# A decoder-mixer kernel whose instruction order a list scheduler sets: VectorE and GpSimd take turns at SBUF in its plan, the last two G blocks run side by side over k, and the first output chunk is split ahead of the last output weights

## The chip, the core and the metric

The kernel runs on one core of a Trainium2 chip. A core has TensorE (PE in the profile; PEld is its weight load), VectorE (DVE), ScalarE (ACT), GpSimd (POOL), and SyncE (SP), which issues transfers; 16 DMA engines move data between HBM and the on-chip memory SBUF. TensorE writes its products to PSUM, eight banks of 128 x 512 floats here. Each engine executes its own instructions strictly in the order in which they stand in the program, and an instruction that waits for another engine holds up everything behind it on its own. The metric is the device time of one execution in microseconds; the median of the timed runs counts.

## The reference, cut to what matters

One layer over x of 1024 tokens by 1024 channels: a normalisation, one input projection, three mixers in parallel, one output projection, a second normalisation, and x added back. All inputs are float32.

```python
h = rms_norm(x, pre_norm_w)
z, xbc, dt_raw, q, f_raw, i_in, g, u, s5_gate = split(h @ w_in)
y_ssd  = ssd_mixer(z, xbc, dt_raw, ...)     # conv, 8 chunks of 128 tokens, 16 heads, gate by silu(z)
y_hgrn = hgrn2_mixer(q, f_raw, i_in, g, ..) # gated linear recurrence, 4 heads, gate by silu(g)
y_s5   = s5_mixer(u, s5_gate, ...)          # complex diagonal state space, then y @ glu_w, rms_norm
mix = concatenate([y_ssd, y_hgrn, y_s5])    # 1024 + 512 + 512 channels
x = x + rms_norm(mix @ w_out, post_norm_w)
```

## The kernel before

**Products.** The large matrix products are done in split precision: `split` (line 305) rounds a float32 tile to a high part on ScalarE (`act`, Copy) and subtracts to get a low part (`sub`), on GpSimd for weights and on VectorE for most others; `mm3` then issues three matmuls (high x high, high x low, low x high). Names of tiles begin with their pool: `r` (16 tiles) holds the normalised input `hh`, `hl` (high and low for eight k blocks), and later the first output weights; `v` (8 half tiles) holds split projection weights, and later the split mixer outputs; `w` holds raw weights; `s` the late weights; `x`, `m`, `h` are work tiles; `p` and `c` are the PSUM banks, four each, taken in turn. Projections write `p` banks, the mixers' small products write `c` banks.

**Stages.** `begin` (351) loads and splits the input and makes the sum of its squares (VectorE adds eight tiles into `m_111`; a matmul with `ones` then sums over partitions). The string `PLAN` (1405) emits in program order the projections (`u`, `x`, `a`, `g`, `z`), values (`v`), HGRN heads (`h`), S5 batches (`s`, with `o` the second half of one) and SSD chunks (`c`). Then follow the S5 output product `s5_glu`, the remaining `z` and `g` projections, and the output stage. In `stage_xbc` (519) the convolution is three `scalar_tensor_tensor` on VectorE (`x<-x,conv_w,x`, 128x1023, 128x1022 and 128x1021). In `s5_core` (978) VectorE runs eight scans, then two products (`pr`, and one half of `pi`) while GpSimd does the other half of `pi` (64x1016), and one add; `s5_emit` (1021) multiplies the result on TensorE.

**The end.** `stage_g2(2)` (487) makes the last two G blocks, each for the two halves n of the tokens: for every n first all eight k of the one block, then of the other. Each half goes through silu to `gs_d` in HBM and is read back in `out_gate` (1271). Then `wout` (751) loads, scales and splits the first eight output weights into the `r` tiles that held `hh` and `hl`: a copy on ScalarE and a `scalar_tensor_tensor` on VectorE each. `out_final` (1278) does one chunk of 128 tokens: it splits four half tiles (gated HGRN, rows 8 of w_out; S5, rows 12; the two halves of SSD, rows 0 and 4) into `v` tiles, each followed by its products with both column halves.

**What sets the order.** Nothing is executed in the order in which it is emitted. Each engine handle is wrapped (`Engine`, line 30; its helper makes line 38 the line of every instruction in the profile), so that `book` records all instructions. `depends` (105) finds which step needs which, and `arrange` (145) plays the program through with a length for each step (`Step`, 73): among all engines it always takes the step that can begin first, and of those that are ready the one with the highest rank; a switch of the matmul kind or of the activation table lowers the rank. It writes down the order on each engine, and `force` makes that the order of the program. So a length in `Step` that is wrong for the chip never makes a wrong result, but puts an instruction ahead of others that could have run while it waits. The plan of before charges a VectorE step `150 + n / 0.96` ns and a GpSimd step `120 + 2.3 * n` ns for n elements per partition, whatever the other engine does.

## Time and profile before

| | |
|---|---|
| median of the timed runs | 921.29 us |
| profiled execution, whole | 916.63 us |
| its span, first to last instruction | 914.7 us |
| mean granted TensorE clock | 0.988 |
| matmuls in the trace | 5857 |
| bytes read from and written to HBM | 89.52 MB, 34.18 MB |

The profile divides the span by engine (share of it in which the engine works), tells for each wait who ended it, and lists instructions in order of time. Nearly all instructions have line 38, so groups are told apart by the tiles that they write and read. A busy TensorE is what limits this kernel for most of the span; its idle time, and the stretches in which its clock was granted at less than 1, are what an order can change.

### The profile page before, as it was taken

The numbers are of one execution on the slowest core, as the hardware profiler recorded it, in microseconds if no ns is written. First come the engines' busy times: TensorE is split into PE (matmuls) and PEld (weight loads), VectorE is DVE, ScalarE is ACT, GpSimd is POOL, SyncE is SP. The second block draws the span as 40 slices with busy tenths as digits, with TensorE's granted clock in tenths as the row PEclk, the third lists the DMA queues.
The fourth block names the chain that finished last, engine by engine and source line by source line (L and its number), as shares of the span: only waits on it lengthen the run. The fifth ranks groups of instructions, "written<-read, shape, count | busy, mean of one in ns | idle before, by whom it ended". The sixth has DMA issues, their size and how long they took to land.

```text
span 914.7 us, 14969 instructions
## 1 busy us (share of the span) xinstructions
PE 865.6 (95%) x5857; PEld 713.3 (78%) x5857; DVE 615.4 (67%) x1069; ACT 380.8 (42%) x626; POOL 278.3 (30%) x232
## 2 busy tenths in 40 slices
PE   7999999898999989799998999999999799999997
PEld 5678878788978868578876877778878688888886
DVE  6997668978157589886857286796466755554531
ACT  5432434343134433254164786736354622222210
POOL 2551222553151135512423153452143231111100
PEclk9999999999999999999999999999999999999999
DMA  8132011472222422245556685778565744343200
GB/s 285 24 110 70 26 48 59 119 241 67 52 79 79 128 78 87 80 122 163 167 168 195 209 292 164 237 214 296 186 200 152 233 163 128 133 138 108 88 34 29
DMA packets 92792, 124.68 MB, mean 136 GB/s; under 512 B 9457, under 2 KB 65457, under 8 KB 92722
## 3 DMA queue, kind: packets, MB, share of 16 engines
q1 hardware_dynamic: 81634, 99.02, 34.4%
q10 hardware_dynamic: 11088, 24.71, 9.0%
q8 instruction: 46, 0.75, 0.3%
q14 instruction: 24, 0.20, 0.1%
HBM read 89.52 MB, written 34.18 MB: 135 GB/s over the span
## 4 chain that ended last, share of the span: by engine, by line
PE 43%; DVE 5%; ACT 2%; DMA 1%; issue 1%; POOL 0%; SPq 0%; DVEq 0%; ACTq 0%; POOLq 0%
PE p L38 32%; PE c L38 11%; DVE m L38 3%; DVE r L38 1%; DMA m<-na_d 1%; DMA m<-us_d 1%; ACT m L38 1%; DVE x L38 0%; DVE h L38 0%; ACT L38 0%; POOL h L38 0%; SPq L38 0%; ACT x L38 0%; ACT h L38 0%; DMA ys_d<-m 0%
## 5 line engine op out<-in xcount | busy, mean ns | idle before, releaser
L38 PE MATMUL p<-r,v 128*128 128x512 f32 (+1 forms) x2280 | 551.4, 395 | 7.6 <-ACT r L38 5.8
L38 PEld LDWEIGHTS p<-r,v 128*128 128x128 f32 x2280 | 420.4, 189 | 97.0 <-issue 6.1
L38 POOL TENSOR_TENSOR v<-w,v 128x512 fp32r<-128x512 f32 x76 | 109.6, 1445 | 218.7 <-ACT v L38 203.4
L38 ACT ACTIVATE v<-w 128x512 fp32r<-128x512 f32 x84 | 52.5, 631 | 174.5 <-PE p L38 163.1
L38 DVE TENSOR_TENSOR m<-m,m 128x512 f32<-128x512 f32 (+7 forms) x107 | 95.8, 918 | 9.9 <-POOL m L38 2.3
L38 PE MATMUL p<-s,v 128*128 128x512 f32 (+1 forms) x408 | 94.5, 389 | 4.9 <-DVE v L38 3.7
L38 PEld LDWEIGHTS c<-m,m 128*32 128x32 f32 (+2 forms) x1904 | 64.4, 129 | 36.2 <-DVE m L38 21.9
L38 PEld LDWEIGHTS p<-s,v 128*128 128x128 f32 x408 | 75.5, 194 | 20.4 <-DVE v L38 4.1
L38 PE MATMUL c<-m,m 128*32 128x16 f32 (+3 forms) x1904 | 70.3, 214 | 22.1 <-DVE m L38 16.7
L38 DVE TENSOR_TENSOR x<-p,rsb 128x512 f32<-128x512 f32 x64 | 47.0, 735 | 42.7 <-PE p L38 42.3
L38 ACT ACT_TABLE_LOAD x46 | 59.0, 1283 | 6.7 <-PE c L38 2.1
L38 DVE SCALAR_TENSOR_TENSOR x<-x,conv_w,x 128x1023 f32<-128x1023 f32 (+2 forms) x36 | 54.6, 1520 | 5.5 <-ACT x L38 4.9
L38 PE MATMUL p<-y,r 128*128 128x272 f32 (+1 forms) x384 | 48.5, 286 | 3.0 <-DVE x L38 1.6
L38 PEld LDWEIGHTS p<-y,r 128*128 128x128 f32 x384 | 47.6, 190 | 3.8 <-DVE x L38 1.8
L38 ACT ACTIVATE x<-x 128x1024 f32<-128x1024 f32 (+1 forms) x30 | 30.1, 1004 | 35.2 <-DVE x L38 30.6
L38 ACT ACTIVATE m<-m,acol 128x128 f32<-128x128 f32 x128 | 40.5, 392 | 8.7 <-DMA ys_d<-m 4.3
L38 DVE TENSOR_TENSOR v<-x,v 128x512 fp32r<-128x512 f32 x24 | 19.1, 801 | 36.7 <-ACT v L38 36.7
L38 PE MATMUL c<-s,s 128*128 128x512 f32 x192 | 43.7, 389 | 0.0
L38 ACT ACTIVATE v<-x 128x512 fp32r<-128x512 f32 x24 | 15.2, 633 | 64.9 <-PE p L38 64.9
L38 PEld LDWEIGHTS c<-s,s 128*128 128x128 f32 x192 | 36.0, 188 | 7.5
L38 POOL TENSOR_TENSOR x<-x,h 128x512 f32<-128x512 f32 x12 | 19.7, 1648 | 72.8 <-DMA h<-gs_d 24.4
L38 ACT ACTIVATE m<-m 128x1024 f32<-128x1024 f32 (+2 forms) x34 | 34.5, 1015 | 15.0 <-DVE m L38 10.8
(181 smaller groups left out, 932.9 us busy)
## 6 DMA issues: line engine op xcount, KB each, us to landing
w<-in_w_in ACTq DMA_DIRECT2D x38, 512.0 KB, 3.7
m<-na_d SPq DMA_DIRECT2D x16, 512.0 KB, 5.2
xc_d<-x SPq DMA_DIRECT2D x12, 512.0 KB, 3.3
q<-in_w_out SPq DMA_DIRECT2D x12, 512.0 KB, 3.7
m<-tb_d SPq DMA_DIRECT2D x16, 256.0 KB, 4.3
m<-xc_d SPq DMA_DIRECT2D x8, 512.0 KB, 5.1
zc_d<-x SPq DMA_DIRECT2D x8, 512.0 KB, 5.2
ym_d<-m SPq DMA_DIRECT2D x8, 512.0 KB, 3.5
```

Of the source, the lines that this page charges most:

```text
L38: made = f(*args, **kw)
```

## The change

There are three parts.

1. **The plan's costs and its port rule.** A step is marked `port` if it is a GpSimd instruction other than a memset, or a VectorE instruction with no source in PSUM. A marked step that would begin more than 100 ns after a marked step of the other engine began, and more than 130 ns before that one ends, is put off in the plan until 130 ns before that end. Lengths change a little too: two-input ScalarE steps under 512 elements +80 ns, VectorE steps that read a scalar per partition beside a tensor of more than 32 elements +65 ns, GpSimd `130 + 2.27 * n`; and 60 ns instead of 100 ns pass until another engine can use a result.
2. **`stage_g2`**: both blocks run side by side over k, in two banks.
3. **`out_split`**: the splitting of a chunk is a generator of its own. It takes S5 first, HGRN second. For chunk 0 it is emitted ahead of the eight `wout`, for the others where it was.

```diff
             elif self.eng == "Pool":
-                self.len = 100 + n / 0.96 if ins.opcode == "Memset" else 120 + 2.3 * n
+                self.len = 100 + n / 0.96 if ins.opcode == "Memset" else 130 + 2.27 * n
+                self.port = ins.opcode != "Memset"
             else:
-                self.len = 150 + n / 0.96
+                self.len = 150 + n / 0.96 + (65 if ins.opcode == "TensorScalarPtr" and len(srcs) > 1 and size(ins.ins[0]) > 32 else 0)
+                self.port = not any(str(x.tensor.space) == "PSUM" for x in srcs)
...
+            t0 = t
+            if s.port:
+
+                b, c = port["Pool" if e == "DVE" else "DVE"]
+                if b + 100 < t < c - 130:
+                    t = c - 130
+                port[e] = (t0, t + s.len)
             now[e] = t + s.len
...
         for n in range(2):
-            for i in range(2):
-                ps = ring("p")
-                for k in range(KD):
-                    whv, wlv = [c3(t)[:, k % 4] for t in ws[i][k // 4]]
+            pss = [ring("p"), ring("p")]
+            for k in range(KD):
+                for ps, w in zip(pss, ws):
+                    whv, wlv = [c3(t)[:, k % 4] for t in w[k // 4]]
                     mm3(ps, whv, wlv, hh[k][:, HS[n]], hl[k][:, HS[n]], k == 0, k == KD - 1)
+            for i, ps in enumerate(pss):
...
+    def out_split(y, hs):
+
+        for x, k0 in ((hs[:, HS[1]], 12), (hs[:, HS[0]], 8), (y[:, HS[0]], 0), (y[:, HS[1]], 4)):
+            h, l = get("v"), get("v")
+            split(x, h, l, V)
+            yield h, l, k0
...
-        srcs = ((hs[:, HS[0]], 8), (hs[:, HS[1]], 12), (y[:, HS[0]], 0), (y[:, HS[1]], 4))
...
+        source, parts = parts or out_split(y, hs), []
...
     out_gate(0, nxt[1])
+    parts = list(out_split(*nxt))
     for t in zip(hh, hl):
         free(*t)
     for k in range(8):
         w[k] = wout(k, "r", mixw[:, k:k + 1], "wq"[k % 2])
```

No instruction is added or taken away on TensorE, VectorE, GpSimd or SyncE; ScalarE has one more table load (47 for 46). But the order differs on every engine. Three places follow.

VectorE at the start of the program, before. `r_81` to `r_91` are the low parts of the input's k blocks, which TensorE waits for; `m_111` takes the sum of squares, which only the matmul with `ones` needs.

```order
L38 SCALAR_TENSOR_TENSOR r_83<-m_114,pre_w,r_82 128x1024
L38 TENSOR_TENSOR v_97<-w_74,v_96 128x512
L38 TENSOR_TENSOR m_111<-m_111,m_112 128x1024
L38 TENSOR_TENSOR v_99<-w_75,v_98 128x512
L38 TENSOR_TENSOR m_111<-m_111,m_113 128x1024
L38 SCALAR_TENSOR_TENSOR r_85<-m_115,pre_w,r_84 128x1024
L38 SCALAR_TENSOR_TENSOR r_87<-m_116,pre_w,r_86 128x1024
```

The same after:

```order
L38 SCALAR_TENSOR_TENSOR r_83<-m_114,pre_w,r_82 128x1024
L38 TENSOR_TENSOR v_97<-w_74,v_96 128x512
L38 TENSOR_TENSOR v_99<-w_75,v_98 128x512
L38 SCALAR_TENSOR_TENSOR r_85<-m_115,pre_w,r_84 128x1024
L38 SCALAR_TENSOR_TENSOR r_87<-m_116,pre_w,r_86 128x1024
L38 TENSOR_TENSOR m_111<-m_111,m_112 128x1024
```

The two sums have moved behind `r_85` and `r_87`; on TensorE the matmul that needs all sums, `c_140<-m_111,ones`, has 19 more projection matmuls ahead of it.

VectorE in the second S5 batch, before, from the scans' product (`m_115<-m_111,m_118`) to the add that TensorE waits for (`m_115<-m_115,m_112`). `x_71<-x_70,conv_w` is a convolution, `x_72<-p` the way of a projection out of PSUM.

```order
L38 TENSOR_TENSOR m_115<-m_111,m_118 128x8x127
L38 SCALAR_TENSOR_TENSOR x_71<-x_70,conv_w,x_71 128x1023
L38 TENSOR_TENSOR x_72<-p_134,rsb 128x512
L38 SCALAR_TENSOR_TENSOR x_71<-x_70,conv_w,x_71 128x1022
L38 SCALAR_TENSOR_TENSOR m_112<-m_124,m_118 64x8x127
L38 TENSOR_TENSOR x_72<-p_135,rsb 128x512
L38 TENSOR_TENSOR m_115<-m_115,m_112 128x1024
```

The same after:

```order
L38 TENSOR_TENSOR m_115<-m_111,m_118 128x8x127
L38 SCALAR_TENSOR_TENSOR x_73<-x_72,conv_w,x_73 128x1023
L38 SCALAR_TENSOR_TENSOR m_112<-m_124,m_118 64x8x127
L38 TENSOR_TENSOR x_69<-p_136,rsb 128x512
L38 TENSOR_TENSOR m_115<-m_115,m_112 128x1024
```

Between the product and the add stand two other instructions instead of four; the convolution into `x_71` now comes ahead of the whole batch. On TensorE the matmul of the result, `c_140<-m_115,m_2316`, has 34 more projection matmuls ahead of it.

ScalarE at the change to the output stage, before. `r_76` to `r_86` are output weights (`wout`); `v_96<-x_70` and `v_92<-x_70` split chunk 0's S5 and HGRN halves, `v_94` and `v_98` its SSD halves.

```order
L38 ACTIVATE v_96<-x_70 128x512
L38 ACTIVATE r_76<-w_75,mix_w 128x1024
L38 ACTIVATE x_73<-x_73 128x512
L38 ACTIVATE r_78<-q_5450,mix_w 128x1024
L38 ACTIVATE r_80<-w_74,mix_w 128x1024
L38 ACTIVATE r_82<-q_5451,mix_w 128x1024
L38 ACTIVATE r_86<-q_5452,mix_w 128x1024
L38 ACTIVATE v_92<-x_70 128x512
```

The same after, where `v_92<-x_70` is the S5 half and `v_96<-x_70` the HGRN half:

```order
L38 ACTIVATE r_76<-w_75,mix_w 128x1024
L38 ACTIVATE v_92<-x_70 128x512
L38 ACTIVATE v_94<-x_69 128x512
L38 ACTIVATE r_78<-q_5450,mix_w 128x1024
L38 ACTIVATE r_80<-w_74,mix_w 128x1024
L38 ACTIVATE r_82<-q_5451,mix_w 128x1024
L38 ACTIVATE r_86<-q_5452,mix_w 128x1024
L38 ACTIVATE v_98<-x_69 128x512
L38 ACTIVATE r_84<-w_75,mix_w 128x1024
L38 ACTIVATE x_73<-x_73 128x512
L38 ACTIVATE r_90<-q_5450,mix_w 128x1024
L38 ACTIVATE v_96<-x_70 128x512
```

The split for the first products stands second instead of behind five weights. VectorE's half of it, `v_93<-x_70,v_92`, stands behind one `r` weight instead of five. On TensorE, two more projection blocks (48 matmuls) stand ahead of `s5_glu` than before, so fewer are left between it and the output stage: 146 rows instead of 196.

## Prediction

> **What bounds the kernel now.** I read the page's head first, then busy time and clock in stretches cut where TensorE stops, then the waits, then the order of time around the two dearest stops.

> ```profile
> span 914.7 us, 14969 instructions
> PE 865.6 (95%) x5857; PEld 713.3 (78%) x5857; DVE 615.4 (67%) x1069; ACT 380.8 (42%) x626; POOL 278.3 (30%) x232
> ```

> TensorE is busy for 865.6 of 914.7 us, and the change leaves its matmuls alone. So the most that can be won is its idle time, 49.1 us, and what a lowered clock costs. The stretches show where both lie (columns: PE, PEld, DVE, ACT and POOL busy, then PEclk, the granted clock).

> ```profile
> core 0: us, PE busy (x) PEld busy (x) DVE busy (x) ACT busy (x) POOL busy (x), PEclk, DMA share, GB/s
> 6.00:80.00 74.00, 67.09 (x319) 54.59 (x320) 70.12 (x146) 32.42 (x44) 33.75 (x26) 0.98 0.42 135
> 160.00:176.00 16.00, 13.12 (x71) 10.61 (x70) 15.65 (x30) 4.67 (x11) 11.66 (x9) 0.89 0.30 87
> 215.00:240.00 25.00, 21.76 (x183) 21.56 (x183) 14.02 (x22) 6.18 (x10) 4.32 (x2) 1.00 0.18 56
> 240.00:300.00 60.00, 58.54 (x647) 47.71 (x647) 33.21 (x53) 22.70 (x36) 20.95 (x20) 1.00 0.24 66
> 300.00:345.00 45.00, 40.61 (x201) 34.54 (x200) 33.82 (x60) 17.30 (x20) 12.45 (x14) 0.96 0.36 107
> 345.00:395.00 50.00, 45.07 (x541) 35.68 (x540) 45.81 (x71) 18.07 (x27) 25.89 (x24) 1.00 0.29 85
> 450.00:485.00 35.00, 33.03 (x188) 26.54 (x186) 23.87 (x35) 17.14 (x27) 9.79 (x9) 1.00 0.53 172
> 485.00:505.00 20.00, 17.25 (x92) 14.84 (x89) 12.79 (x20) 11.95 (x25) 7.98 (x4) 0.91 0.56 170
> 505.00:640.00 135.00, 133.88 (x825) 105.51 (x824) 92.22 (x165) 89.83 (x177) 51.30 (x38) 1.00 0.74 235
> 640.00:715.00 75.00, 73.73 (x320) 59.77 (x320) 42.72 (x47) 33.11 (x43) 20.10 (x14) 1.00 0.61 185
> 715.00:745.00 30.00, 25.08 (x97) 19.84 (x96) 23.11 (x24) 15.35 (x19) 11.65 (x6) 0.89 0.72 239
> 745.00:908.00 163.00, 163.00 (x764) 136.92 (x763) 74.57 (x145) 38.39 (x83) 19.82 (x16) 1.00 0.28 92
> ```

> From 745 to 908 us TensorE never stops: the output stage has nothing to win. Ahead of it, idle time in these rows (length less PE) is 6.91, 2.88, 3.24, 1.46, 4.39, 4.93, 1.97, 2.75, 1.12, 1.27 and 4.92: 35.8 us. The clock's loss (length times 1 less PEclk) is 1.5, 1.8, 1.8, 1.8 and 3.3 us in the rows under 1.00: 10.2 us, always in a row where TensorE stopped. Together 46 us, 5% of the span. Who ended the stops:

> ```profile
> PE c L38 <- DVE m L38: 19.9, 12, 4.4
> PE p L38 <- DVE v L38: 3.7, 1, 3.7
> PE p L38 <- ACT v L38: 1.3, 1, 1.3
> PE p L38 <- DVE r L38: 0.9, 1, 0.9
> ```

> Mostly VectorE. Why it is late is seen in the order of time at the second S5 batch:

> ```profile
> 320.82 7.42 PE L38 MATMUL p<-r,v 128*128 128x512 f32 x32
> 322.81 3.36 POOL L38 TENSOR_TENSOR m<-m,m 64x1016 f32<-64x1016 f32 x1 [1.36 <-issue]
> 323.85 3.41 DVE L38 SCALAR_TENSOR_TENSOR x<-x,conv_w,x 128x1023 f32<-128x1023 f32 x1
> 327.78 1.70 DVE L38 SCALAR_TENSOR_TENSOR x<-x,conv_w,x 128x1022 f32<-128x1022 f32 x1
> 331.35 1.22 DVE L38 TENSOR_TENSOR m<-m,m 128x1024 f32<-128x1024 f32 x1
> 332.62 1.65 PE L38 MATMUL c<-m,m 128*128 128x128 f32 x6 [4.39 <-DVE m L38]
> ...
> L38 DVE SCALAR_TENSOR_TENSOR x<-x,conv_w,x 128x1021 f32<-128x1021 f32 x12 | 15.4, 1280 | 0.3
> ```

> The convolution's step takes 1.28 us for almost the same size in the group's row, but 3.41 us here: GpSimd began at 322.81 and ended at 326.17, and VectorE's instruction ended 1.09 us behind it. It was held until GpSimd was done. The plan of before did not know that; it took the add (331.35) to come 2.1 us earlier (3.41 less 1.28), and put the matmul that needs it ahead of others that were ready. The clock then falls.

> **Part 1, the plan, stretch by stretch.** One projection matmul costs TensorE 0.227 us:

> ```profile
> 799.93 21.78 PE p L38 x96
> ```

> A stop goes where the plan puts more matmuls ahead of the waiting one than it lasts, unless VectorE's result comes later too.

> - 6 to 80 us (8.4 with clock): the matmul with `ones` gets 19 matmuls, 4.3 us, against this wait of 2.12 us, and `r_85`, the wait of 0.9 us above, comes two adds earlier (one of them took 2.91 us, held by GpSimd):

> ```profile
> 34.52 2.02 PE L38 MATMUL c<-m,ones 128*128 128x512 f32 x3 [2.12 <-DVE m L38]
> 15.83 2.91 DVE L38 TENSOR_TENSOR m<-m,m 128x1024 f32<-128x1024 f32 x1
> ```

>   That takes 2.1 + 0.9 and the clock's 1.5. Of the other 3.9 I take half, since VectorE is full (70.1 of 74 us): -6.5.
> - 160 to 176: the waiting matmul moves back by 72 others (16.3 us against 2.9): -4.6 with the clock.
> - 215 to 240: the exception. The waiting matmul comes 16 value matmuls earlier, and a convolution still stands behind GpSimd's 64x1016 step. One convolution fewer is worth 1.3 us on VectorE, 16 value matmuls (7.96 / 65 = 0.122 us each) 2.0 us: +0.7.

> ```profile
> 213.76 7.96 PE L38 MATMUL p<-y,r 128*128 128x256 f32 x65
> ```

> - 240 to 300: 15 matmuls (3.4 us) against 1.46: -1.5.
> - 300 to 345: 34 matmuls (7.7 us), but TensorE arrives earlier by what the rows above save. VectorE's chain loses the 1.70 us convolution; the other still meets GpSimd. I leave a wait of 1.0 without a fall of the clock: -5.2.
> - 345 to 395: only 2 to 13 matmuls more, and VectorE busy for 45.8 of 50 us: half, -2.4.
> - 450 to 485 and 485 to 505: 29 and 30 matmuls (6.6 us) against 1.97 and 2.75: -1.4 and, with the clock, -4.0.
> - 505 to 640 and 640 to 715: 23 and 55 matmuls against waits of about 1: -0.6 and -0.9.

> **The clock.** Its five falls lie right behind five of the stops, three of them of 2.1 to 2.9 us, so I let all 10.2 us go with the stops (6.9 of them here). [...]

> Sum of part 1: -26.4 us. More filler is used early, and 50 rows fewer (11.4 us) stand between the S5 product and the output stage; the cover that is lost there is part 2's matter.

> **Parts 2 and 3, the change to the output stage.**

> ```profile
> 718.90 1.99 DVE L38 SCALAR_TENSOR_TENSOR r<-w,mix_w,r 128x1024 fp32r<-128x1024 f32 x1 [0.58 <-ACT r L38]
> 723.46 0.61 ACT L38 ACTIVATE v<-x 128x512 fp32r<-128x512 f32 x1
> 724.12 1.20 PE L38 MATMUL p<-s,v 128*128 128x512 f32 x4 [1.25 <-ACT v L38]
> 725.87 2.47 DVE L38 SCALAR_TENSOR_TENSOR r<-q,mix_w,r 128x1024 fp32r<-128x1024 f32 x2
> 728.25 0.68 DVE L38 TENSOR_TENSOR v<-x,v 128x512 fp32r<-128x512 f32 x1
> 728.99 1.22 PE L38 MATMUL p<-s,v 128*128 128x512 f32 x2 [3.67 <-DVE v L38]
> ```

> TensorE waits 1.25 us for ScalarE's split and 3.67 us for VectorE's, which stand behind five output weights. Afterwards they stand behind one. The `v` tiles that they write are free when half of the k blocks of the second pair are done, 24 matmuls (5.4 us) ahead of the first product; ScalarE's 0.61 and VectorE's 0.68 fit there. The weights can begin earlier too: side by side, `r_76` is last read 42 matmuls ahead of the pair's end, not 24 (4.1 us). The HGRN half now follows seven weights on ScalarE and is needed 24 matmuls after the first product; with VectorE's share (1.24 us a weight in the row of two, 1.99 in the first) I leave 1.5 us. The S5 half, now first, was ready long before:

> ```profile
> 689.56 1.67 POOL L38 TENSOR_TENSOR x<-x,h 128x512 f32<-128x512 f32 x1 [2.36 <-DVE h L38]
> ```

> It ends at 691.2, 33 us ahead of the first output product at 724.1; the 11.4 us of cover lost above leave 21. So of 4.92 + 3.3 us, 6.7 go. The additional table load (below, 1.28 us) lies on ScalarE, 42% busy, ahead of chunk 1's gate, which has 73 matmuls of cover: nothing.

> ```profile
> L38 ACT ACT_TABLE_LOAD x46 | 59.0, 1283 | 6.7 <-PE c L38 2.1 <-PEq L1471 1.7 <-DVE x L38 0.9
> ```

> **What comes back.** Where TensorE no longer waits it arrives earlier at the next result, and the plan leaves no reserve: it takes the first step that is ready. What new waits cost no row shows. At the least nothing; at the most they come back in all stretches where VectorE is full (6 to 80, 160 to 176, 300 to 395), 18.7 of the 33.1 us. I take 7, four new waits of the mean of `DVE m` above (19.9 / 12 = 1.7): nearer to the low end, since the plan now has the lengths that the rows show.

> **The sum.** -26.4 - 6.7 + 7 = -26 us: a span of 889. The profiled execution took 916.63, 1.9 more than its span; the median, 921.29, is 4.7 above that, and I keep both: 889 + 1.9 + 4.7 = 895 us, 2.9% less.

> **The rivals.**
> - *The stops move instead of going.* VectorE is the bound in the stretches just named; a matmul put back meets a result that is as late. For it: 15.65 of 16 us busy there. Against: VectorE rests for 33% of the span, and what it defers (S5 parameters, convolutions) is not urgent. Price: those 18.7 us and half of the 7 again; 921.3 - 33.1 + 18.7 + 3.5 = 910. Within 2%.
> - *The clock still falls.* If its falls hang on something else than these stops, 10.2 us stay: 905, within 2%. For it: the 3.24 us stop shows 1.00, a shorter one (2.75) 0.91. Against: no stretch without a stop shows a fall.
> - *The plan's rule doesn't bite:* GpSimd delays VectorE in too few places and the order is merely different. Then only parts 2 and 3 count: 921.3 - 6.7 = 915.
> - *Slower: projection weights come late.* Their low parts are GpSimd's:

> ```profile
> L38 POOL TENSOR_TENSOR v<-w,v 128x512 fp32r<-128x512 f32 x76 | 109.6, 1445 | 218.7 <-ACT v L38 203.4
> ```

>   The plan now puts GpSimd off behind VectorE. A weight half has 12 to 24 matmuls (2.7 to 5.4 us) of cover. If each of 76 came 0.7 us beyond it, 53 us against 33 gained: 941. It decides from 0.6 us on average (46 us, so 18 more than before, 2%). Against: no row of TensorE's waits names `POOL v`, and GpSimd is 30% busy.

> **How the numbers follow.** My forecast 0.62; stops move 0.19; clock still falls 0.08; the rule doesn't bite 0.07; slower 0.04. A measurement of this kernel tells about 2% from no change, so faster means under 902.9. All of the first, a fifth of the second and a quarter of the third lie there: 0.68; same 0.28; slower 0.04. The likeliest case alone spans 883 (nothing comes back, 888, and the halves that I left in two stretches go too) to 902 (all 7 twice). The range for 8 in 10 reaches to the case in which the stops move: 882 to 912.

> **What would show it.** Right: idle time of TensorE ahead of the output stage under 20 us; no PEclk under 1.00 around 170, 330 and 495; a wait of 3 to 4 us near 215 still there; the first output product without a wait. Wrong in part 1: as many `DVE m` waits as before, only later. Wrong in parts 2 and 3: a wait for `v` at the first products, or for the `ones` sums behind the S5 product. The whole fails if GpSimd's weight parts appear among TensorE's waits.

## The result, and the profile after

The changed kernel takes 888.63 us (median of 4 runs, 886.83 to 890.83) against 921.26 for the kernel before: ratio 0.9662, 95% interval 0.9617 to 0.9706. That is 3.4% faster. One run of the kernel before took 1387.61 us, and the ratio, which is one of means, leaves it out. The forecast was 895 (882 to 912). The profiled execution took 890.83 us, 1.83 more than its span of 889.0.

First the head of the profile after (busy time of each engine, its share of the span, and its instructions):

```profile
span 889.0 us, 14989 instructions
PE 860.1 (97%) x5857; PEld 708.6 (80%) x5857; DVE 615.9 (69%) x1069; ACT 380.9 (43%) x627; POOL 276.0 (31%) x232
```

The work is the same. TensorE's idle time fell from 49.1 to 28.9 us. The same stretches as in the prediction, with the same columns (PE, PEld, DVE, ACT and POOL busy, then PEclk):

```profile
6.00:80.00 74.00, 67.06 (x321) 55.57 (x321) 63.93 (x126) 32.93 (x44) 36.88 (x26) 0.95 0.40 134
160.00:176.00 16.00, 16.00 (x79) 13.42 (x78) 15.09 (x34) 5.69 (x11) 11.02 (x10) 1.00 0.47 152
215.00:240.00 25.00, 24.43 (x178) 23.24 (x179) 14.04 (x20) 10.79 (x15) 3.06 (x3) 1.00 0.33 91
240.00:300.00 60.00, 60.00 (x654) 48.90 (x653) 38.60 (x56) 26.79 (x40) 19.16 (x20) 1.00 0.29 89
300.00:345.00 45.00, 44.31 (x220) 37.26 (x220) 39.76 (x71) 18.73 (x21) 16.13 (x18) 1.00 0.31 97
345.00:395.00 50.00, 50.00 (x590) 40.93 (x589) 40.48 (x72) 17.67 (x29) 20.22 (x23) 1.00 0.36 98
450.00:485.00 35.00, 32.83 (x192) 26.44 (x192) 23.73 (x35) 22.95 (x43) 12.25 (x7) 1.00 0.54 167
485.00:505.00 20.00, 19.49 (x99) 15.79 (x98) 6.58 (x10) 16.64 (x30) 3.88 (x3) 1.00 0.67 225
505.00:640.00 135.00, 133.48 (x810) 104.11 (x809) 97.86 (x165) 80.60 (x161) 48.99 (x36) 1.00 0.72 228
640.00:715.00 75.00, 72.02 (x300) 57.60 (x299) 53.33 (x57) 39.87 (x49) 21.70 (x15) 0.95 0.71 220
715.00:745.00 30.00, 30.00 (x134) 24.83 (x133) 20.28 (x33) 8.91 (x18) 8.48 (x7) 1.00 0.49 155
```

Idle time plus the clock's loss (length times 1 less PEclk), in us, beside the prediction's terms. The transition to the output stage has moved from 715–745 into the row ahead, so the last two rows are taken together.

| stretch | before | after | change | predicted |
|---|---|---|---|---|
| 6–80 | 8.4 | 10.6 | +2.2 | -6.5 |
| 160–176 | 4.6 | 0 | -4.6 | -4.6 |
| 215–240 | 3.2 | 0.6 | -2.7 | +0.7 |
| 240–300 | 1.5 | 0 | -1.5 | -1.5 |
| 300–345 | 6.2 | 0.7 | -5.5 | -5.2 |
| 345–395 | 4.9 | 0 | -4.9 | -2.4 |
| 450–485 | 2.0 | 2.2 | +0.2 | -1.4 |
| 485–505 | 4.6 | 0.5 | -4.0 | -4.0 |
| 505–640 | 1.1 | 1.5 | +0.4 | -0.6 |
| 640–745 | 9.5 | 6.7 | -2.8 | -7.6 |
| sum | 46.0 | 22.8 | -23.2 | -33.1, and +7 |

The gain lies between 160 and 505 us. At the start nothing was won, and at the transition less than half of what was expected. The span fell by 25.7 us: 20.2 idle time, 2.7 clock (10.2 to 7.5), and 2.8 in the time that TensorE is busy without the clock's loss (865.6 less 10.2, against 860.1 less 7.5).

The 2.7 us of clock are those of this pair of executions. Each run lists its span and mean clock, and the span times 1 less the clock is counted as what the clock costs it. The profiled execution of before, at 0.988, lost 11.0 us so, less than any of the 46 runs of that kernel in the groups below: they have 0.978 to 0.986 and lose 12.8 to 20.3 us, 16.5 on average. The four runs of the changed kernel lose 4.4 to 7.1, 5.5 on average. Over the runs, then, the mean span falls by 30.4 us (917.3 to 886.9), of which 11 are clock.

The waits of TensorE after (sum, times, longest, in us), without the first wait of the program, 5.6 us, and one of 0.2:

```profile
PE c L38 <- DVE m L38: 8.2, 6, 3.8
PE p L38 <- DVE m L38: 3.1, 1, 3.1
PE p L38 <- ACT v L38: 1.9, 1, 1.9
PE c L38 <- DVE h L38: 1.5, 2, 1.2
PE c L38 <- DMA m<-us_d: 1.5, 1, 1.5
PE p L38 <- DVE v L38: 0.9, 1, 0.9
```

Twelve waits of 19.9 us for VectorE's `m` became six of 8.2, and 3.8 of these is one stop at the start. The four S5 batches had stops of 3.24, 4.39, 1.75 and 2.75 us; they have 0.92, 0.69, 1.52 and none. How a stop went is seen in the order of time at the second S5 batch (start, length, instruction; in brackets the wait ahead of it):

```profile
319.09 3.36 POOL L38 TENSOR_TENSOR m<-m,m 64x1016 f32<-64x1016 f32 x1 [1.36 <-issue]
320.12 3.40 DVE L38 SCALAR_TENSOR_TENSOR x<-x,conv_w,x 128x1023 f32<-128x1023 f32 x1
321.81 5.15 PE L38 MATMUL p<-r,v 128*128 128x512 f32 x22
326.38 1.22 DVE L38 TENSOR_TENSOR m<-m,m 128x1024 f32<-128x1024 f32 x1
327.65 0.60 PE L38 MATMUL c<-m,m 128*128 128x128 f32 x3 [0.69 <-DVE m L38]
```

VectorE is held exactly as before: the convolution takes 3.40 us behind GpSimd's product (3.41 before). But TensorE now has projection matmuls (`p<-r,v`) ahead of the result, and waits 0.69 us instead of 4.39. The rule does not remove the contention; it makes the plan count on it.

The two places that are left, first the start:

```profile
25.49 12.94 DVE L38 TENSOR_TENSOR m<-m,m 128x1024 f32<-128x1024 f32 x6
25.65 2.81 POOL L38 TENSOR_TENSOR m<-m 128x1024 f32<-128x1024 f32 x1 [2.36 <-DVE r L38]
28.43 8.93 POOL L38 TENSOR_TENSOR v<-w,v 128x512 fp32r<-128x512 f32 x4
38.49 3.56 PE L38 MATMUL c<-m,ones 128*128 128x512 f32 x4 [3.83 <-DVE m L38]
```

Six adds take 2.16 us each (12.94 / 6; one alone takes 1.22, above), and GpSimd's four weight parts 2.23 (8.93 / 4): each is held by the other. Then the transition:

```profile
703.73 1.88 POOL L38 TENSOR_TENSOR x<-x,h 128x512 f32<-128x512 f32 x1 [2.19 <-DMA h<-gs_d]
705.64 0.63 ACT L38 ACTIVATE v<-x 128x512 fp32r<-128x512 f32 x1 [1.81 <-POOL x L38]
706.32 1.27 PE L38 MATMUL p<-s,v 128*128 128x512 f32 x4 [1.93 <-ACT v L38]
708.45 7.48 PE L38 MATMUL p<-s,v 128*128 128x512 f32 x20 [0.86 <-DVE v L38]
```

Chunk 0's HGRN half is late by 1.93 and 0.86 us, not because of ScalarE's weights ahead of its split but because the gate's read from HBM lands only then (GpSimd's product waits 2.19 us for it). The first output products (S5) do not wait.

### The profile page after: what moved, and what is told of

It is laid out like the page before. It is cut to its first block, busy times and chain, and to the rows that moved or that the text cites. A ratio compares the mean times of both kernels' runs of the same rounds, so it can differ in the third digit from the quotient of the medians.

```text
span 889.0 us, 14989 instructions
## 1 busy us (share of the span) xinstructions
PE 860.1 (97%) x5857; PEld 708.6 (80%) x5857; DVE 615.9 (69%) x1069; ACT 380.9 (43%) x627; POOL 276.0 (31%) x232
## 4 chain that ended last, share of the span: by engine, by line
PE 81%; DVE 12%; DMA 4%; issue 2%; ACT 1%; POOL 0%; SPq 0%; DVEq 0%; POOLq 0%; ACTq 0%
PE p L38 61%; PE c L38 19%; DVE m L38 6%; DVE x L38 2%; DMA m<-in_xT 1%; DVE r L38 1%; DMA h<-ea_d 1%; DVE h L38 1%; DMA w<-in_w_out 1%; DVE v L38 1%; DMA m<-us_d 1%; ACT h L38 0%; DVE rsb L38 0%; ACT L38 0%; ACT x L38 0%
## 5 line engine op out<-in xcount | busy, mean ns | idle before, releaser
L38 PE MATMUL p<-r,v 128*128 128x512 f32 (+1 forms) x2280 | 554.6, 396 | 8.7 <-ACT r L38 5.6
L38 PEld LDWEIGHTS p<-r,v 128*128 128x128 f32 x2280 | 419.9, 189 | 98.2 <-issue 6.2
L38 POOL TENSOR_TENSOR v<-w,v 128x512 fp32r<-128x512 f32 x76 | 113.9, 1501 | 200.2 <-ACT v L38 176.8
L38 ACT ACTIVATE v<-w 128x512 fp32r<-128x512 f32 x84 | 52.7, 630 | 170.5 <-PE p L38 160.9
L38 DVE TENSOR_TENSOR m<-m,m 128x512 f32<-128x512 f32 (+7 forms) x107 | 98.3, 943 | 13.4 <-PE c L38 4.3
L38 PE MATMUL p<-s,v 128*128 128x512 f32 (+1 forms) x408 | 94.5, 388 | 2.8 <-ACT v L38 1.9
L38 PEld LDWEIGHTS p<-s,v 128*128 128x128 f32 x408 | 75.3, 193 | 18.4 <-ACT v L38 2.3
L38 PEld LDWEIGHTS c<-m,m 128*32 128x32 f32 (+2 forms) x1904 | 61.2, 127 | 18.5 <-DVE m L38 8.8
L38 PE MATMUL c<-m,m 128*32 128x16 f32 (+3 forms) x1904 | 66.8, 210 | 4.6 <-DVE m L38 3.1
L38 DVE TENSOR_TENSOR x<-p,rsb 128x512 f32<-128x512 f32 x64 | 46.7, 736 | 34.5 <-PE p L38 33.8
L38 ACT ACT_TABLE_LOAD x47 | 60.3, 1283 | 10.5 <-POOL v L38 4.0
L38 DVE SCALAR_TENSOR_TENSOR x<-x,conv_w,x 128x1023 f32<-128x1023 f32 (+2 forms) x36 | 57.4, 1600 | 5.3 <-ACT x L38 4.8
L38 PE MATMUL p<-y,r 128*128 128x272 f32 (+1 forms) x384 | 47.7, 286 | 0.0
L38 PEld LDWEIGHTS p<-y,r 128*128 128x128 f32 x384 | 47.5, 190 | 0.2
L38 PE MATMUL c<-s,s 128*128 128x512 f32 x192 | 43.7, 389 | 0.0
L38 ACT ACTIVATE m<-m,acol 128x128 f32<-128x128 f32 x128 | 40.1, 390 | 5.7 <-DMA m<-na_d 2.6
L38 PEld LDWEIGHTS c<-s,s 128*128 128x128 f32 x192 | 36.0, 188 | 7.5
L38 ACT ACTIVATE v<-x 128x512 fp32r<-128x512 f32 x24 | 14.9, 630 | 56.6 <-PE p L38 50.4
L38 DVE TENSOR_TENSOR v<-x,v 128x512 fp32r<-128x512 f32 x24 | 19.2, 808 | 26.3 <-ACT v L38 26.3
L38 POOL TENSOR_TENSOR x<-x,h 128x512 f32<-128x512 f32 x12 | 16.8, 1403 | 65.3 <-DMA h<-gs_d 37.1
L38 ACT ACTIVATE m<-m 128x1024 f32<-128x1024 f32 (+2 forms) x34 | 34.4, 1011 | 5.5 <-DVE r L38 4.9
L38 ACT ACTIVATE x<-x 128x1024 f32<-128x1024 f32 (+1 forms) x30 | 29.9, 1001 | 15.4 <-DVE x L38 15.2
```

The lines of the kernel that those rows point to most:

```text
L38: made = f(*args, **kw)
```

## The experiments

Each was run beside the kernel before on the same chip; the medians of before were 918.60, 918.97, 921.01 and 918.91 us in the four groups. Ratios are to before. The changed kernel was not run again in them, so a difference taken against its 888.63 us is one between groups, and the medians of before differ by up to 2.7 us between groups. In the rows quoted below, stretch 80–640 holds the mixers, 640–760 the transition.

### Which part carries the gain

**Part 1 alone (`plan_only`).** The diff's classes `Step` and function `arrange`, with `stage_g2` and the output stage as before.

> The new lengths and the port rule, with the G blocks one after the other and chunk 0 split after its weights, as before. Theory (part 1 carries the gain; the terms were -26.4 for it, less some of the 7 that comes back): 895 to 905 us, TensorE's stops between 80 and 640 us gone, the two waits for v ahead of the first output product (1.25 and 3.67 us) and the fall of the clock behind them still there. Rival (the rule does not bite, the end carries the gain): 912 us or more, with stops of 2 to 4 us behind VectorE's m adds near 165 and 330 us.

897.74 us, ratio 0.9764 (0.9743 to 0.9786). Its stretches:

```profile
80.00:640.00 560.00, 552.77 (x4450) 454.02 (x4449) 412.71 (x717) 264.14 (x442) 193.06 (x166) 1.00 0.47 144
640.00:760.00 120.00, 109.22 (x460) 88.28 (x459) 76.19 (x101) 51.28 (x73) 32.26 (x23) 0.94 0.55 175
```

The changed kernel and the one before, in the same stretches, in that order:

```profile
80.00:640.00 560.00, 552.68 (x4455) 454.31 (x4454) 416.31 (x723) 264.38 (x443) 193.92 (x166) 1.00 0.47 143
640.00:760.00 120.00, 117.02 (x499) 94.85 (x498) 82.00 (x107) 52.08 (x75) 32.56 (x24) 0.97 0.62 196
```

```profile
80.00:640.00 560.00, 535.79 (x4359) 441.47 (x4359) 401.30 (x696) 257.68 (x433) 192.62 (x164) 0.99 0.45 137
640.00:760.00 120.00, 113.81 (x482) 92.04 (x482) 75.76 (x91) 53.42 (x72) 35.47 (x23) 0.97 0.59 187
```

The plan alone does all there is between 80 and 640 us (552.77 against 552.68; 535.79 before). At the transition it loses 4.6 us of TensorE's time against before, and 0.03 of the clock: the waits of 1.25 and 3.67 us, which were expected to stay, became one of 5.40 for ScalarE's `v` and one of 5.18 for the sum of a norm (`c<-h,ones`).

**Parts 2 and 3 alone (`end_only`).** The diff without `Step` and `arrange`.

> The plan of before (no port rule, old lengths), with the G blocks side by side and chunk 0 split first. Theory: 912 to 917 us (the prediction's 6.7 us for this part against 921.3, somewhat less by the trace of the changed kernel); the m stops stay, the first output product does not wait for v. Rival (the end carries the gain): under 900 us.

919.37 us, ratio 1.0000 (0.9983 to 1.0017): nothing, where the prediction had 6.7 and the expectation 912 to 917. The first product no longer waits, but the work behind it now does:

```profile
734.75 1.22 PE L38 MATMUL c<-h,ones 128*128 128x256 f32 x2 [2.99 <-DVE h L38]
737.05 2.08 PE L38 MATMUL p<-s,v 128*128 128x512 f32 x4 [1.08 <-ACT v L38]
```

The sum for chunk 1's SSD norm (`c<-h,ones`) and the HGRN half stand still for 4.07 us, where TensorE had stood 4.92 for the splits of the first products. The wait was turned into another.

**Part 2 undone (`g_serial`), the early place of part 3 undone (`split_late`; S5 still comes first).** In the changed kernel:

```diff
 g_serial, stage_g2:
-            pss = [ring("p"), ring("p")]
-            for k in range(KD):
-                for ps, w in zip(pss, ws):
+            for i in range(2):
+                ps = ring("p")
+                for k in range(KD):
 split_late:
-    parts = list(out_split(*nxt))
+    parts = None
```

> The changed kernel with part 2 undone: the last two G blocks one after the other again, chunk 0 still split first. Theory of the prediction (side by side only lets the weights begin some 4 us earlier): 889 to 893 us. Rival (it is part 2 that takes the 10 us of stops out of the transition that stay when both parts are undone): 895 to 899 us.

> The changed kernel with part 3's place undone: the G blocks side by side, chunk 0 split behind the eight weights. Theory of the prediction (the split is what the first output products waited for): 894 to 898 us, waits for v of 4 to 6 us at the first products. Rival (part 2 alone does it): 888 to 891 us.

888.60 (ratio 0.9677, 0.9637 to 0.9717) and 897.95 us (0.9771, 0.9737 to 0.9805). Part 2 is worth nothing here that stands out of the spread of the runs (887.4 to 890.5 without it, 886.8 to 890.8 with it). With chunk 0 split late TensorE does not wait for `v`, as the theory said, but in one stop of 9.33 us for the sum of chunk 1's norm (`c<-h,ones`), whose VectorE steps stand among the output weights. The early split is worth 9.3 us, but only with the new plan, since without it (`end_only`) both parts together are worth nothing. The parts do not add.

### Which part of the plan

**No port rule (`no_port`); the rule with the old lengths (`port_only`).**

```diff
 no_port:
-                self.port = ins.opcode != "Memset"
+                self.port = False
-                self.port = not any(str(x.tensor.space) == "PSUM" for x in srcs)
+                self.port = False
 port_only: the lengths and the 100 ns of before
```

> The changed kernel without the port rule; its new lengths stay. Theory (the rule is what moves the matmuls back): 900 to 915 us, stops behind VectorE's m adds near 165 and 330 us are back. Rival (the new lengths and the shorter 60 ns do it): 885 to 893 us, as the changed kernel.

> The changed kernel with the lengths and the 100 ns of before, the port rule kept. Theory (the rule does it): 886 to 897 us. Rival (the lengths do it): 905 us or more.

919.86 us (ratio 1.0008, 0.9989 to 1.0026) and 901.82 (0.9814, 0.9793 to 0.9835). Without the rule the whole gain is gone; the theory's 900 to 915 was too low. With the rule and the old lengths the time lies between the theory's range and the rival's 905. The stretches of the kernel without the rule, then of the one with the old lengths:

```profile
80.00:640.00 560.00, 534.31 (x4347) 439.53 (x4346) 400.69 (x702) 252.09 (x427) 194.26 (x164) 0.98 0.43 131
640.00:760.00 120.00, 111.17 (x474) 89.80 (x473) 75.14 (x87) 57.91 (x74) 30.96 (x22) 0.96 0.62 207
```

```profile
80.00:640.00 560.00, 553.49 (x4460) 456.61 (x4460) 408.76 (x727) 264.08 (x440) 199.89 (x168) 1.00 0.46 138
640.00:760.00 120.00, 107.08 (x450) 85.65 (x449) 82.17 (x101) 53.54 (x74) 26.58 (x21) 0.94 0.61 198
```

Between 80 and 640 us the rule is everything: 534.31 without it, 553.49 with it and the old lengths. That is no chance of one order: all nine kernels with the rule have 552.2 to 556.6 there, and the three without it and without a reserve (before, `end_only`, `no_port`) 534.3 to 535.8. The 13 us that separate `port_only` from the changed kernel all lie at the transition (107.08 against 117.02, and 3.6 us of clock). Every change of the plan deals the order there anew, and the transition has no matmuls to spare; whether the new lengths are better there, or that deal was only lucky, these runs don't tell.

**A reserve in place of the rule (`reserve`).** `no_port`, and 1000 ns instead of 60 until another engine can use a result of VectorE or GpSimd. The expectation names TensorE too; its 200 ns in fact stayed.

> The changed kernel without the port rule; in its place the plan lets 1000 ns instead of 60 pass until another engine can use a result of VectorE, GpSimd or TensorE (TensorE had 200). Theory (the plan must know where VectorE is held; a general reserve also delays results that are in time): 900 to 915 us. Rival (any reserve moves the matmuls back far enough): 885 to 895 us.

921.26 us, ratio 1.0027 (1.0010 to 1.0044). This is above the theory's range. Slack everywhere is no substitute for the whole: TensorE stood still for 7.8 us at the start and for 17.4 in three waits for ScalarE's `v`, of which 6.18 and 9.40 at the transition. But between 80 and 640 us it is busy for 545.57 us, against 535.79 before and 552.68 in the changed kernel: there the reserve did more than half of what the rule does. Whether it would have paid with a better order at the two ends was not tried.

### Whether GpSimd is what holds VectorE

**GpSimd's S5 product cut (`before_cut`).** The kernel of before, every instruction at its old place (one line more, not shown, keeps the plan's lengths); part of the S5 state is left out.

```diff
         for o in (pr, pi):
-            G.memset(g3(o)[:, :, 0:1], 0.0)
+            G.memset(g3(o)[:, :, 0:P - 1 if o is pi else 1], 0.0)
...
-        mul(G, g3(pi)[IM, :, rest], g3(st)[RE, :, before], rv[RE, :, before])
+        mul(G, g3(pi)[IM, :, P - 1:P], g3(st)[RE, :, P - 2:P - 1], rv[RE, :, P - 2:P - 1])
```

> The kernel of before with its order kept on every engine. GpSimd's 64x1016 product in each S5 batch writes only one column of 127 per group (64x8); a memset fills the rest with zeros, so part of the S5 state is left out. Theory (VectorE is held until GpSimd's step ends): the convolution at 323.85 us takes 1.28 us instead of 3.41, the stop of 4.39 us at 328 shrinks to 2.0 to 2.6 and the clock does not fall behind it, the one of 3.24 at 221 to about 1; 910 to 916 us in all. Rival (the 3.41 us have another cause, such as the transfers that run there): the convolution still takes about 3.4 us, 917 to 920 us.

909.52 us, ratio 0.9888 (0.9850 to 0.9926). At the second S5 batch:

```profile
323.89 1.20 POOL L38 TENSOR_TENSOR m<-m,m 64x8 f32<-64x8 f32 x1 [1.36 <-issue]
324.93 1.28 DVE L38 SCALAR_TENSOR_TENSOR x<-x,conv_w,x 128x1023 f32<-128x1023 f32 x1
326.49 1.29 POOL L38 TENSOR_TENSOR v<-w,v 128x512 fp32r<-128x512 f32 x1 [1.40 <-ACT v L38]
326.72 2.14 DVE L38 SCALAR_TENSOR_TENSOR x<-x,conv_w,x 128x1022 f32<-128x1022 f32 x1
332.02 1.16 PE L38 MATMUL c<-m,m 128*128 128x128 f32 x8 [2.71 <-DVE m L38]
```

The convolution is back at 1.28 us with nothing but GpSimd's step and its memset changed. The stop at 221 us went from 3.24 to 0.92, as expected; the one at 328 went from 4.39 to 2.71, a little more than expected, since the next convolution now runs into a weight's low part (2.14 us). The clock stayed at 1.00 from 300 to 345 us. The waits for VectorE's `m` fell from 19.9 to 11.3 us. So the diagnosis of the prediction is shown: GpSimd's 64x1016 step held VectorE's (3.41 us beside it, 1.28 without it). The time is just under the expected 910 to 916.

### What is left

**The output halves in another order (`end_order`).**

```diff
-        for x, k0 in ((hs[:, HS[1]], 12), (hs[:, HS[0]], 8), (y[:, HS[0]], 0), (y[:, HS[1]], 4)):
+        for x, k0 in ((hs[:, HS[1]], 12), (y[:, HS[0]], 0), (hs[:, HS[0]], 8), (y[:, HS[1]], 4)):
```

> The changed kernel with the four halves of an output chunk taken in the order S5, first SSD half, HGRN, second SSD half. Theory (the 1.93 and 0.86 us at 704 and the fall of the clock behind them, 3.4 us, come from the read of the silu gate that lands at 703.66; the first SSD half and its four weights are ready by 699): 882 to 884 us, no stop over 1 us between 640 and 720. Rival (the wait moves to the weights of SSD's rows): 888 us or more, with waits for r at the second group of output products.

882.28 us, ratio 0.9600 (0.9566 to 0.9635), and no stop at the transition:

```profile
640.00:715.00 75.00, 74.80 (x327) 60.88 (x326) 55.37 (x61) 40.18 (x51) 25.70 (x19) 1.00 0.71 223
715.00:745.00 30.00, 30.00 (x134) 24.85 (x133) 20.96 (x41) 9.59 (x24) 6.79 (x6) 1.00 0.42 145
```

**The start: a stricter rule (`strict`), or less work on GpSimd (`start_act`).**

```diff
 strict, arrange:
-                if b + 100 < t < c - 130:
+                if b <= t < c - 130:
 start_act, begin and rsqrt:
-            if k % 2:
-                mul(G, xs[k], xs[k], xs[k])
-            else:
-                act(xs[k], xs[k], AF.Square)
+            act(xs[k], xs[k], AF.Square)
...
-        mul(G, z, y, y)
+        if width == D:
+            act(z, y, AF.Square)
+        else:
+            mul(G, z, y, y)
```

> The changed kernel with a port rule that also holds a step which would begin within 100 ns of the other engine's; the sum over ones then gets 20 more projection matmuls ahead of it. Theory (what bounds the start is the chain of adds and of the rsqrt, not the order: the matmuls put ahead are missing behind it): 886 to 892 us, the idle time between 30 and 55 us still 6 to 8 us, only at another place. Rival (the stop at 34.7 us is an error of the plan): 880 to 884 us.

> The changed kernel with all eight squares of the input, and the square inside the first normalisation's rsqrt, on ScalarE; GpSimd has none of them. Theory (the two stops of 3.83 and 3.11 us at 34.7 and 48.7 us are VectorE's adds and rsqrt steps held behind GpSimd, 2.16 us an add for 1.22): 881 to 885 us, each of the two stops under 2 us and one fall of the clock fewer before 60 us. Rival (the stops are bound by the chain from the last input tile to rsb and by ScalarE, which now also delays the split weights): 887 to 892 us.

886.48 us (ratio 0.9649, 0.9617 to 0.9681) and 879.61 (0.9556, 0.9526 to 0.9586). From 30 to 56 us the changed kernel, `strict` and `start_act`, in that order:

```profile
30.00:56.00 26.00, 19.06 (x66) 13.66 (x65) 22.80 (x28) 11.98 (x17) 17.99 (x13) 0.87 0.28 82
```

```profile
30.00:56.00 26.00, 19.01 (x69) 14.47 (x68) 24.69 (x32) 13.17 (x18) 19.89 (x13) 0.80 0.37 100
```

```profile
30.00:56.00 26.00, 26.00 (x122) 21.25 (x122) 23.00 (x38) 14.93 (x20) 18.68 (x19) 1.00 0.40 113
```

In `strict` the stop at the sum over `ones` is gone and one of 6.99 us stands nine matmuls behind it, at the first that needs a freed bank: the idle time is the same 7 us. This order did not help there: the matmuls that were put ahead are missing behind the sum, until VectorE's `rsb` lets a bank go. In `start_act` the adds take 1.22 to 1.28 us, the sum runs at 29.82 us instead of 38.49, and TensorE does not stop between there and 80 us; the time is better than the expected 881 to 885. Which of its two edits does it was not tried apart, and the order changes with them.

**Both (`both`).** `end_order` and `start_act` together.

> The changed kernel with the order S5, first SSD half, HGRN, second SSD half and with the start's squares on ScalarE. Theory (the two gains lie at different places and add): 873 to 879 us. Rival (the order of the whole shifts and one of the gains is lost): 881 us or more.

874.29 us, ratio 0.9504 (0.9470 to 0.9538): 14.3 us less than the changed kernel's 888.63 and within the expected range; the two gains taken alone are 6.4 and 9.0. TensorE is busy for 852.9 of 872.7 us. This version is faster than the kernel before and the changed one.

## Why the prediction was right

**The diagnosis** was right, and is shown: VectorE held behind GpSimd (3.41 us, and 1.28 in `before_cut`), and a plan that did not know it (`no_port`). Of the signs that the prediction named, idle time ahead of the output stage (15.4 us in the rows above, under 20), the clock at 170, 330 and 495 us and the first output product came as said; "a wait of 3 to 4 us near 215 still there" did not, it is 0.92.

**Part 1, -26.4 us.** Alone it gave 20.9 us (918.60 to 897.74); the prediction's sum with the 7 that comes back was 19.4. By place it was uneven. Four terms came out within 0.3 us (160, 240, 300 and 485). The two from 450 and from 505 were 1.6 and 1.0 us too hopeful. The third S5 batch still stops, for 1.52 us, now at 445 and so outside the row; inside it a wait of 1.47 for a read from HBM (`us_d`) came up, and in the next row one of 1.22 for VectorE's `h`. Three were off by more:
- *6 to 80 us, -6.5.* "The matmul with `ones` gets 19 matmuls, 4.3 us, against this wait of 2.12 us." It did, but the adds came later as well: the last ended at 34.47 us before and ends at 38.44 now. One add instead of four stands ahead of VectorE's last low part of the input, and the other six run in one block beside GpSimd's square and weight parts, at 2.16 us each instead of 1.22. I priced the filler and not the delay of what it is to fill. The five stops of 0.4 to 1.6 us of this row all went, but the stop of 2.12 became 3.83 and one of 3.11 behind the rsqrt came up. `strict` shows that moving more matmuls ahead does not help here, and `start_act` that less work on GpSimd does; this was the rival "the stops move", and here it holds.
- *215 to 240, +0.7.* VectorE's add came 9.4 us earlier (224.90 to 215.51), and TensorE only 7.1 (221.72 to 214.65). I had counted one convolution, 1.3 us, for VectorE's side, and left the rest of its chain where it was; but the product ahead of it began 8.1 us earlier (216.46 to 208.40). The stop fell by 2.3 us to 0.92.
- *345 to 395, -2.4.* Halving was too careful: all of 4.9 went, although VectorE is still busy for 40.5 of 50 us.

**Parts 2 and 3, -6.7.** The first products no longer wait, as said. "For the HGRN half I leave 1.5 us" became 2.79 and a fall of the clock (3.75 us by the row 640 to 715), by a cause that the prediction did not look at: the gate's way through HBM (`end_order`). "The weights can begin earlier too: side by side" brought nothing (`g_serial`). And the term was taken as independent of part 1, which it is not: 0 without the new plan, about 9 with it (897.74 to 888.63), since part 1 alone makes this place worse, 10.6 us of stops for 4.9.

**The clock.** "I let all 10.2 us go with the stops" was too much in this pair of executions: 7.5 stay, all of them at the two places that still stop. Over the runs the clock gave 11 us, but out of 16.5 (above): the one trace showed less loss than is usual, and the nearness of 10.2 to 11 is luck. Around 170 and 495 us, behind the stops of 2.88 and 2.75 us, all of the loss went with the stops (PEclk 0.89 and 0.91 before, 1.00 in both rows after).

**What comes back, +7.** The table gives 9.9 (33.1 less 23.2), of which the start has 8.7 and the transition 4.8, against better results elsewhere. New waits in the middle are small: 0.2 and 0.4 us more in two stretches, and 0.4 between 395 and 450 us, which the table leaves out. So the size was nearly right, and its place was not: I had shared it among all stretches in which VectorE is full.

**The sum** of 889 for the span was met (889.0), by errors that cancel: that it came out to the microsecond is luck. The 6.4 us between 895 and 888.63 are the last step, "I keep both": the median of before lay 4.7 us above its profiled execution, and the median after lies 2.2 below its own. In the later groups the median of before was 918.6 to 921.0, so a good part of the 4.7 was chance: the profiled execution had a higher clock than any later run of that kernel, and lost 5.5 us less to it than those on average.

**The rivals.** *The rule doesn't bite*: refuted by `no_port`. *Slower by late weights*: no row of TensorE's waits after names `POOL v`. *The stops move*: true at the start alone. *The clock still falls*: in the traces true for three quarters of the loss, over the runs for a third, and only at stops that remain.

## What to carry to other kernels

A list scheduler needs no faster engines to gain, but must know where one engine holds up another (here 3.41 us for 1.28); general slack replaced that only in part of the program. Where a wait is moved, price the delay of the waited-for result as well as the filler put ahead of it, and look for places with no filler to spare: there a shorter chain helped, by the squares on ScalarE and by another order of the halves. Changes of a plan are not independent: measure parts alone and together before adding them. And take the clock's loss from many runs, since one trace shows one draw of it (11.0 us in the profiled execution of before, 16.5 on average over 46 runs of that kernel).

## What the runs showed of the hardware

```profile
32.06:35.47 3.41, 1.29 (x4) 0.49 (x3) 3.41 (x5) 2.28 (x5) 1.21 (x1) 1.00 0.01 2
35.47:38.88 3.41, 3.41 (x7) 2.00 (x6) 3.07 (x15) 2.14 (x5) 1.54 (x3) 0.50 0.00 0
219.80:223.21 3.41, 1.92 (x16) 1.71 (x15) 3.34 (x3) 0.40 (x1) 0.12 (x1) 1.00 0.00 0
223.21:226.62 3.41, 1.67 (x15) 1.67 (x15) 2.98 (x4) 0.43 (x1) 0.95 (x1) 1.00 0.00 0
492.86:496.27 3.41, 1.37 (x12) 1.37 (x13) 3.41 (x3) 2.75 (x3) 0.90 (x1) 1.00 0.76 220
496.27:499.68 3.41, 3.41 (x20) 3.41 (x18) 0.31 (x1) 0.60 (x1) 0.00 (x0) 0.50 0.77 263
```

TensorE busy for 1.29 of 3.41 us, and the next window runs at half speed; the stop of 3.24 us at 221 is shared by two windows (1.92 and 1.67 busy), and nothing follows. The two traces have 485 windows at full clock between 11.5 and 860 us: behind the eight in which TensorE was idle for 56 to 100% the clock fell each time, behind the 477 with 0 to 55% in none. The grid lies differently in the two executions: its lines stand at 1.34 us and every 3.41 us from there in the trace of before, at 0.74 in that of the changed kernel. So a stop cost no clock (the 3.24 us at 221), 1.7 us, half of 3.41 (the 4.39 us at 328), or 3.4, half of 6.83 (the 3.67 us up to 728.99). The four runs of the changed kernel have spans of 889.0, 885.7, 885.0 and 888.0 us at mean clocks of 0.992, 0.995, 0.995 and 0.993, and the span less the clock's loss is 880.6 to 881.9 in all four.

**GpSimd was held by VectorE too.** GpSimd's 128x512 weight part took 1.29 us unhindered (`before_cut`, 326.49) and 2.23 between VectorE's adds in the changed kernel. In `before_cut` GpSimd's 64x8 step took 1.20 us, from 323.89 to 325.09, while VectorE's product ran from 323.79 to 325.01: it ended only behind it. Both engines lost time where their steps met (2.16 us for 1.22 an add, 2.23 for 1.29 a weight part). With the squares taken off GpSimd (`start_act`) VectorE's adds took 1.22 to 1.28 us, and the kernel is 9.0 us faster than the changed one.
